# Hybrid RG-LRU / attention / RWKV-7 block: attention of the later queries first, and the output projection and feed-forward in the order of the later tokens

## Chip, cores and metric

One core of a Trainium2 chip. The metric is the device time in microseconds of one execution of the whole block. Engines: PE (TensorE), DVE (VectorE), ACT (ScalarE), POOL (GpSimd), SP (the queue that issues the DMAs).

## What is computed

One layer over 2048 tokens and 16 learned meta tokens ahead of them, width 1024:

```python
p = rms_norm(h, norm_mix_pre) @ w_in          # columns of three head groups
oa = rg_lru_group(...)                        # 256 columns, a recurrence over time
ob = forgetting_attention_group(q, k, v, f)   # 512 columns: 8 heads of 64, causal, with a decay bias
oc = rwkv7_group(...)                         # 256 columns, a recurrence over time
h = h + rms_norm(concat(oa, ob, oc) @ w_out, norm_mix_post)
f = causal_dwconv3(rms_norm(h, norm_ffn_pre) @ ffn_up); gate, val = split(f)
h = h + rms_norm((gelu(gate) * val) @ ffn_down, norm_ffn_post)
return h[:, 16:]
```

All arithmetic is float32; a product of two matrices is made of three products of split operands (`mm3`, L148 to L152).

## The kernel before

The order of each engine's instructions is set when the program is built: the code below is written in program order, a scheduler interleaves what is independent, and each engine then goes through its list in that order, waiting wherever an input isn't there.

Stages, in program order. The input projection (`psp`) runs with the RWKV and the LRU beside it; the RWKV isn't done when it ends, and goes on beside the attention. Its products are called `rps` and `eps`, and its lines are L898 to L1350.

Attention (`Attn`, L394) writes its queries as **steps**: one step is one head and one block of 512 queries. Block 0 sees 5 key tiles, block 1 sees 9, block 2 sees 13, block 3 sees 17 (the last tile of each has 16 keys, and the four tiles on the diagonal are narrower than 512). `run` (L708) goes through two halves: `half` 0 takes blocks 0 and 1 of all eight heads (short steps), `half` 1 takes blocks 2 and 3 (long steps), and `meta` (L537), the attention of the 16 meta tokens, stands between them. A head's keys (`keys`, L454, its DMAs on L469 to L476) are two float32 parts of the keys and the values. A short head needs 1040 key columns and fills half a slot of the ring of keys, so four short heads fit; a long head needs 2064 and fills a slot, so two fit. For each step, `maxima` (L479) makes the row maxima two steps ahead: PE product `mx` (L503), DVE reductions `mc` (L506, and L509 on the diagonal), then once a step the chain `sh` (L516, L517), a transposition (L521) and `q` (L532). `weights` (L597) then makes, for each pair of key tiles, the scores `sc` (L623, L624), the exponentials `p` on ACT (L626), the product with the values `po` (L635) and the sum `acc` on POOL and DVE (L656), and once a step the division by that sum (L675 to L688) with two trips through DRAM. `mx` has two PSUM banks, and a third once `wide` is set (`WIDE`, from head 5 of the first half).

The output projection (`w_out_tile`, L1377, products `pswo`) goes over 17 tiles of tokens (`FFN_TILES`, L1419: 2 tokens, which are the last meta tokens, then 16 times 128). A tile needs the attention of all heads for its tokens. Tiles 0 to 8 need meta tokens and blocks 0 and 1, tiles 9 to 16 blocks 2 and 3. In program order they stand behind the attention, but the scheduler moves tiles 0 to 6 into the long half. Tiles 7 and 8 (`HELD`) are kept until the last step but one. Each tile has one chain of small DVE operations (L84 to L89), L1412 and L1413 on DVE, and writes `scr_h`. From the ninth tile (`LATE`) each is followed by `ffn_norm` (L1440) of one tile of the first third of the feed-forward (products `pst`, copies L55 and L57), and after the last of these `ffn_sums` (L1473, 16 POOL subtractions on L1479) and the splits `xo` of its first three operands (L1484 on ACT, L1485 on DVE).

The up-projection (`ffn_up`, L1567, products `psu`) goes over three thirds of the tokens (`SUPERS`), 0, 1, 2, each with 22 column blocks; `between` (L1964) prepares the next third meanwhile. The down-projection (`psd`) goes over the tokens from the first to the last.

Of the kernel before, what the change touches and what calls it, by code (L numbers as in the profile page):

```python
# [29 lines left out]
NFF = FF // P  # L30
# [363 lines left out]
class Attn:  # L394
# [313 lines left out]
    def run(self):  # L708


        ready, self.steps = [], []
        for half, bs in enumerate(((0, 1), (2, 3))):
            if half:
                self.meta()
            for h in range(NH):
                self.wide = (half, h) >= WIDE
                keys = self.keys(h, 4 * bs[-1] + 5)
                for b in bs:
                    gen, total, out = self.maxima(h, b, keys), self.pieces(b), []

                    def fill(share, gen=gen, total=total, out=out):
                        while len(out) < min(total, share * total):
                            out.append(next(gen))

                    if len(ready) == self.AHEAD:
                        self.weights(*ready.pop(0), fill)
                        self.steps.append(self.last)
                    fill(1.0)
                    ready.append((h, b, keys, next(gen)))
        for step in ready:  # L730
            self.weights(*step, lambda share: None)
            self.steps.append(self.last)
        for _, _, f in self.later:
            f()
# [684 lines left out]
FFN_TILES = [(0, HALO)] + [(HALO + P * i, P) for i in range(SEQ // P)]  # L1419
# [2 lines left out]
HK = KD // 2  # L1422
SUPERS = 3

# [37 lines left out]
def ffn_quarters(core, pool, sup):  # L1462

    t = pool.tile([P, len(QUARTERS), HK, FN], F32, tag="q", name=core.n("q"))
    q = {s: t[:, i] for i, s in enumerate(QUARTERS)}
    used = SEQ + HALO - FBLK * (2 * sup + 1)
    if used < FN:
        for s in ("b0", "b1"):
            core.nc.gpsimd.memset(q[s][:, :, used:], 0.0)
    return q  # L1470


def ffn_sums(core, q, after=nullcontext):  # L1473

    q["t3"] = q["b0"]
    for k in range(HK):
        for o, x, y in (("t1", "b0", "a0"), ("t2", "b1", "t1"), ("t3", "b1", "b0"), ("t4", "a1", "t2")):
            with after():
                core.nc.gpsimd.tensor_tensor(q[o][:, k], q[x][:, k], q[y][:, k], op=ALU.subtract)  # L1479
            yield  # L1480
# [86 lines left out]
def ffn_up(core, raws, ring, pool, banks, w_up, cw, scr, between, tokens):  # L1567

    nc = core.nc
    tt, stt = nc.vector.tensor_tensor, nc.vector.scalar_tensor_tensor
    turn = 0
    units = [(sup, j) for sup in range(SUPERS) for j in range(NFF)]
    ahead = UpWeights(core, raws, ring, w_up, scr, 0)
    ws = [ahead.operand(i) for i in range(7)]
    xs = [tokens(0, i) for i in range(7)]

    def conv(src, u, j, n):
        y = pool.tile([P, FBLK], F32, tag="uy", name=core.n("uy"), bufs=UY)  # L1580
        cc = u * NFF + j
        nc.scalar.activation(y[:, :n], src[:, 2 : n + 2], AF.Copy, scale=cw[:, 88 + cc : 89 + cc])  # L1582
        for i in (1, 0):
            stt(y[:, :n], src[:, i : n + i], cw[:, 44 * i + cc : 44 * i + cc + 1], y[:, :n], op0=ALU.mult, op1=ALU.add)  # L1584
        if u == 0:
            nc.scalar.activation(y[:, :n], y[:, :n], AF.Gelu_apprx_tanh)
        return y

    def ending(g, v, j, b0, n):
        core.pooled = nc.gpsimd.tensor_tensor(v[:, :n], g[:, :n], v[:, :n], op=ALU.mult)  # L1590
        nc.sync.dma_start(scr["ff"][P * j : P * j + P, b0 : b0 + n], v[:, :n])

    for at, (sup, j) in enumerate(units):
        b0 = [FBLK * (2 * sup + i) for i in range(2)]
        n = [min(FBLK, SEQ - b) for b in b0]
        s = lambda tag: pool.tile([P, FN], F32, tag=tag, name=core.n(tag), bufs=1 if tag == "u2" else 2)[:]
        between(sup, j)
        more = at + 1 < len(units)
        if more:
            ahead = UpWeights(core, raws, ring, w_up, scr, units[at + 1][1])  # L1600
        ws_next, bank = [], {}
        turn ^= 1
        for i, (name, (_, _, at_)) in enumerate(PRODUCTS.items()):
            w, x = ws[i], xs[i]
            first = at_ not in bank
            if first:
                bank[at_] = banks[turn].tile([P, 512], F32, tag="up", name=core.n("psu"))[:, :FN]
            ps = bank[at_]
            for k in range(HK):
                mm3(nc, ps, w[:, 0, k], w[:, 1, k], x[:, 0, k], x[:, 1, k], first and k == 0, k == HK - 1, not first)  # L1610
            if j == NFF - 1 and more:
                xs[i] = tokens(sup + 1, i)
# [24 lines left out]
        ws = ws_next  # L1637
# [132 lines left out]
READY = 13  # L1770
PACE = 1.5

WIDE = (0, 5)

LATE = 8

HELD = 7, 8


class Beside:  # L1780
# [54 lines left out]
def hybrid_block_kernel(ctx: ExitStack, tc: tile.TileContext, args, out):  # L1835
    a = {s: v[0] if s != "meta_tokens" else v for s, v in args.items()}
    nc = tc.nc
    core = Core(tc, ctx)
    scr = scratch(tc, ctx, core)
# [4 lines left out]
    def run(gen):  # L1844
        for _ in gen:
            pass
# [78 lines left out]
    with ExitStack() as p3:  # L1925
# [12 lines left out]
        with p2:  # L1938
            ps_wo.append(pool(p2, "ps_wo2", 1, space=PSUM, **right))
            banks = Banks(core, ps_wo)  # L1940
            g_post = spread(pool(p2, "gpost", 1, **right), a["norm_mix_post"], "g_post")
            wp = pool(p2, "wp", 2, **right)
            w = w_out_load(core, wp, a["w_out"])
            todo = list(tiles[0])
            quarters = {0: ffn_quarters(core, qp, 0)}
            for i, (f, rows) in enumerate(FFN_TILES):
                with tc.issue_after(at.steps[-2].ins) if i in HELD else nullcontext():
                    _, rs[i] = w_out_tile(
                        core, wp, banks, scr, w, x, meta, g_post, f + META - HALO, rows, rsv[:, 6 * i : 6 * i + 6]
                    )  # L1950
                banks.wide = i >= LATE - 1
                if i >= LATE and todo:
                    q, f, rows = todo.pop(0)
                    ffn_norm(core, np_, ps_n, scr, f, rows, rs[q], g_fpre, quarters[0], 0)
                    if not todo:
                        run(ffn_sums(core, quarters[0]))
# [6 lines left out]

        def between(sup, j):  # L1964

            sup += 1
            if j == 1 and sup < SUPERS:
                quarters[sup] = ffn_quarters(core, qp, sup)
                todo[:] = tiles[sup]
            elif j == 1:  # L1970
                kept = qp.tile([P, DOWN_KEPT, 2, 512], F32R, tag="q", name=core.n("qd"))
                down.extend(kept[:, i] for i in range(DOWN_KEPT))
            elif sup == SUPERS:
# [89 lines left out]
```

## Time and profile before

| | |
|---|---|
| median of 3 runs | 3165.64 us (3157.63 to 3165.91) |
| the profiled execution | 3168.61 us, of it 3166.9 us span of the trace |
| granted TensorE clock | 0.958 |
| PE, DVE, ACT, POOL busy | 2955.7, 2196.1, 1446.3, 1274.0 us |
| input projection, first part of the RWKV | 0 to 918 us |
| attention beside the rest of the RWKV | 918 to 1228 us |
| attention, with output projection | 1228 to 1500 us |
| attention alone | 1500 to 1640 us |
| end of the attention, rest of the output projection | 1640 to 1795 us |
| up-projection | 1795 to 2670 us |
| down-projection | 2670 to 3167 us |

The stages are read from where the products of each name begin and end on PE. In the lines of the profile, `x` is a count, and what stands in brackets behind an instruction is how long its engine was idle ahead of it and who ended that.

### The profile page before, as it was taken

Reading aid. Unit: us, or ns where it says so; the run is one execution under the profiler, and the core shown is the slowest. Engines: PE = TensorE matmul, PEld = TensorE weight load, DVE = VectorE, ACT = ScalarE, POOL = GpSimd, SP = SyncE. Lnnn points to the kernel's source line nnn. Section 1 sums busy time; section 2 is a strip of 40 time slices with the busy share of each in tenths; the row PEclk is TensorE's granted clock in tenths of the full one; section 3 lists DMA queues with packets and bytes.
Section 4 is the critical chain, followed back from the end, with each engine's and each line's share of the span. In section 5 each row is a group of like instructions: output and inputs, shape, how many; then the busy total and the mean of one; then the engine's idle time right before and its main releaser. Section 6 shows DMA issues by size and latency. Waiting matters only on the chain. (4 is left out here: it accounts for less than half of the span.)

```text
span 3166.9 us, 52619 instructions
## 1 busy us (share of the span) xinstructions
PE 2955.7 (93%) x18488; PEld 2473.9 (78%) x18488; DVE 2196.1 (69%) x4563; ACT 1446.3 (46%) x2684; POOL 1274.0 (40%) x1426
## 2 busy tenths in 40 slices
PE   6988899999989998999999899999999999999998
PEld 6977788889965554554457699999999999787776
DVE  6147665766677777766657777787778787557777
ACT  3134323444444443434543456666666665324332
POOL 3334334211013444434651235433533334556665
PEclk9989899999987998999999899999999999999999
DMA  6777756643453344444326365555555565535444
GB/s 194 225 235 229 220 181 215 200 125 111 116 126 68 81 100 123 119 109 116 77 61 206 115 190 168 167 173 168 165 165 164 168 189 159 177 103 170 140 160 140
DMA packets 493817, 484.11 MB, mean 153 GB/s; under 512 B 83200, under 2 KB 408010, under 8 KB 487904
## 3 DMA queue, kind: packets, MB, share of 16 engines
q1 hardware_dynamic: 493168, 480.36, 50.8%
q8 instruction: 145, 2.38, 0.3%
q14 instruction: 120, 0.98, 0.1%
q0 software_dynamic: 384, 0.39, 0.0%
HBM read 354.76 MB, written 125.87 MB: 152 GB/s over the span
## 5 line engine op out<-in xcount | busy, mean ns | idle before, releaser
L150 PE MATMUL psu<-xo,uw 128*128 128x344 f32 x1848 | 588.7, 323 | 7.9 <-DVE wx L1413 4.8
L151 PE MATMUL psu<-xo,uw 128*128 128x344 f32 x1848 | 593.7, 322 | 1.0 <-DVE xo L1485 1.0
L152 PE MATMUL psu<-xo,uw 128*128 128x344 f32 x1848 | 583.0, 320 | 0.0
L150 PE MATMUL psp<-xh,wh 128*128 128x384 f32 (+2 forms) x1152 | 386.0, 335 | 0.0
L152 PE MATMUL psp<-xh,wl 128*128 128x384 f32 (+2 forms) x1152 | 382.1, 332 | 3.0 <-DVE wl L145 3.0
L151 PE MATMUL psp<-xl,wh 128*128 128x384 f32 (+2 forms) x1152 | 383.0, 332 | 0.0
L150 PEld LDWEIGHTS psu<-xo,uw 128*128 128x128 f32 x1848 | 347.5, 189 | 9.4 <-DVE wx L1413 5.2
L151 PEld LDWEIGHTS psu<-xo,uw 128*128 128x128 f32 x1848 | 348.9, 189 | 1.3 <-DVE xo L1485 1.3
L152 PEld LDWEIGHTS psu<-xo,uw 128*128 128x128 f32 x1848 | 347.2, 189 | 0.0
L1484 ACT ACTIVATE uw<-uq 128x512 fp32r<-128x512 f32 x462 | 287.0, 627 | 99.1 <-PE psu L152 48.0
L1485 DVE TENSOR_TENSOR uw<-uq,uw 128x512 fp32r<-128x512 f32 x330 | 283.2, 862 | 63.5 <-ACT uw L1484 58.6
L626 ACT ACTIVATE p<-sc,bias 128x512 f32<-128x512 f32 (+4 forms) x352 | 201.1, 592 | 267.8 <-PE sc L624 211.7
L1485 POOL TENSOR_TENSOR uw<-uq,uw 128x512 fp32r<-128x512 f32 x132 | 182.4, 1382 | 267.2 <-ACT uw L1484 233.8
L656 POOL TENSOR_TENSOR acc<-acc,p 128x512 f32<-128x512 f32 (+3 forms) x208 | 226.6, 1090 | 153.2 <-ACT p L626 118.8
L1584 DVE SCALAR_TENSOR_TENSOR uy<-psu,ffn_cols,uy 128x342 f32<-128x342 f32 (+1 forms) x396 | 224.2, 569 | 90.0 <-ACT uy L1582 88.9
L1590 POOL TENSOR_TENSOR uy<-uy,uy 128x342 f32<-128x342 f32 (+1 forms) x132 | 137.0, 1038 | 322.0 <-DVE uy L1584 133.9
L506 DVE TENSOR_REDUCE mc<-mx 128x1 f32<-128x400 f32 (+6 forms) x320 | 172.5, 554 | 93.4 <-PE mx L503 89.2
L152 PEld LDWEIGHTS psp<-xh,wl 128*128 128x128 f32 x1152 | 222.6, 193 | 10.3 <-issue 4.5
L150 PEld LDWEIGHTS psp<-xh,wh 128*128 128x128 f32 x1152 | 222.6, 193 | 8.8 <-issue 6.5
L151 PEld LDWEIGHTS psp<-xl,wh 128*128 128x128 f32 x1152 | 222.6, 193 | 6.5 <-issue 4.6
L1503 POOL TENSOR_TENSOR us<-us 128x512 f32<-128x512 f32 x88 | 131.3, 1492 | 222.3 <-DMA us<-in_ffn_up_dram 197.5
L1484 ACT ACTIVATE fo<-u 128x896 fp32r<-128x896 f32 x88 | 81.1, 922 | 234.3 <-POOL u L1700 117.1
(447 smaller groups left out, 6513.7 us busy)
## 6 DMA issues: line engine op xcount, KB each, us to landing
uq<-scr_us SPq DMA_DIRECT2D x264, 256.0 KB
uq<-in_ffn_up_dram SPq DMA_DIRECT2D x198, 256.0 KB
raw<-in_w_in_dram SPq DMA_DIRECT2D x72, 512.0 KB
us<-in_ffn_up_dram SPq DMA_DIRECT2D x44, 512.0 KB
scr_us<-us SPq DMA_DIRECT2D x22, 1024.0 KB
u<-scr_ff SPq DMA_DIRECT2D x88, 256.0 KB
scr_ff<-uy SPq DMA_DIRECT2D x110, 171.0 KB
q<-scr_qh SPq DMA_DIRECT2D x96, 128.0 KB
```

Of the source, the lines that this page charges most:

```text
L150: nc.tensor.matmul(out, ah, bh, start=first, stop=False, skip_group_check=more)
L151: nc.tensor.matmul(out, ah, bl, start=False, stop=False, skip_group_check=more)
L152: nc.tensor.matmul(out, al, bh, start=False, stop=last, skip_group_check=more)
L506: self.reduced = nc.vector.tensor_reduce(mc[:rows, i, ci : ci + 1], ps[:rows, :full], axis=AX.X, op=ALU.max)
L626: last = nc.scalar.activation(p[:rows, :w], ps[:rows, :w], AF.Exp, bias=bias[:rows, j : j + 1])
L656: eng.tensor_tensor(a, ps_[0][:rows, c0:n] if jj == 0 else a, p[:rows, : n - c0], op=ALU.add)
L1484: core.nc.scalar.activation(hi, src, AF.Copy)
L1485: (eng or core.nc.vector).tensor_tensor(lo, src, hi, op=ALU.subtract)
L1503: add, sub = (lambda o, x, y, op=op: nc.gpsimd.tensor_tensor(o, x, y, op=op) for op in (ALU.add, ALU.subtract))
L1584: stt(y[:, :n], src[:, i : n + i], cw[:, 44 * i + cc : 44 * i + cc + 1], y[:, :n], op0=ALU.mult, op1=ALU.add)
L1590: core.pooled = nc.gpsimd.tensor_tensor(v[:, :n], g[:, :n], v[:, :n], op=ALU.mult)
```

## The change

`run` takes the halves in the other order: first blocks 2 and 3 (long steps) of all heads, then the meta tokens, then blocks 0 and 1. The third bank for `mx` is used from the start of the second half. The output projection takes tiles 9 to 16 first, then 0 to 8; the two tiles that are kept for the end of the attention are now 15 and 16. The feed-forward takes its thirds in the order 2, 0, 1, so that the first third needs tiles 11 to 16 (six, where third 0 needs seven). The work, its shapes and the DMAs are the same in number.

```diff
-        for half, bs in enumerate(((0, 1), (2, 3))):
+        for half, bs in enumerate(((2, 3), (0, 1))):
...
+ORDER = 2, 0, 1
...
-    units = [(sup, j) for sup in range(SUPERS) for j in range(NFF)]
+    units = [(sup, j) for sup in ORDER for j in range(NFF)]
...
-WIDE = (0, 5)
+WIDE = (1, 0)
+OUT_ORDER = [9, 10, 11, 12, 13, 14, 15, 16, 0, 1, 2, 3, 4, 5, 6, 7, 8]
 LATE = 8
-HELD = 7, 8
+HELD = 6, 7
...
-            for i, (f, rows) in enumerate(FFN_TILES):
-                with tc.issue_after(at.steps[-2].ins) if i in HELD else nullcontext():
+            for at_, i in enumerate(OUT_ORDER):
+                f, rows = FFN_TILES[i]
+                with tc.issue_after(at.steps[-2].ins) if at_ in HELD else nullcontext():
...
-                if i >= LATE and todo:
+                if at_ >= LATE and todo:
```

What this does to the lists of the engines. First the start of the attention. On SP, before, behind the last stores of the input projection (`k` and `v` are the keys and values of the first head, `q` its queries):

```order
L469 DMA k_1494_10978<-scr_kh 64x1040
L473 DMA k_1493_10977<-scr_kh 64x1040
L474 DMA k_1493_10977<-scr_kl 64x1040
L471 DMA k_1494_10978<-scr_ch 1x1040
L472 DMA k_1494_10978<-scr_cl 1x1040
L475 DMA v_1495_10979<-scr_v 128x8x64
L476 DMA v_1495_10979<-scr_v 16x64
L490 DMA q_1496_10982<-scr_qh 64x512
L491 DMA q_1503_11006<-scr_qh 64x512
```

and now, at the same place:

```order
L469 DMA k_1494_10978<-scr_kh 64x2064
L473 DMA k_1493_10977<-scr_kh 64x2064
L474 DMA k_1493_10977<-scr_kl 64x2064
L471 DMA k_1494_10978<-scr_ch 1x2064
L472 DMA k_1494_10978<-scr_cl 1x2064
L475 DMA v_1495_10979<-scr_v 128x16x64
L476 DMA v_1495_10979<-scr_v 16x64
L490 DMA q_1496_10982<-scr_qh 64x512
L491 DMA q_1503_11006<-scr_qh 64x512
```

The order is the same; the keys and values ahead of the queries are twice as long. On PE at that place, as a difference (`rps` and `eps` are the RWKV's):

```order
 L990 MATMUL eps_8941<-rwsq_8804,bones 128x256
-L623 MATMUL sc_11101<-q_1503_11006,k_1493_10977 128x512
-L623 MATMUL sc_11107<-q_1503_11006,k_1493_10977 128x400
 L1222 MATMUL rps_8429<-ident,rww_903_6518 128x128 x2
 L1226 MATMUL rps_8432<-rwsg_6173,g_up 128x256
+L623 MATMUL sc_11149<-q_1503_11006,k_1493_10977 128x512
+L623 MATMUL sc_11154<-q_1503_11006,k_1493_10977 128x512
```

The first scores stand behind three small products of the RWKV, ahead of which they stood. Second, PE in the middle of the RWKV, around the same two of its products (L1145), before:

```order
L1130 MATMUL rps_10152<-rww_1228_8949,rwxf_9985 64x128 x4
L1145 MATMUL rps_10161<-rwsc_8948,rwxu_10130 64x128 x8
L503 MATMUL mx_11675<-k_1499_10989,q_1501_10993 128x256
L503 MATMUL mx_11680<-k_1499_10989,q_1501_10993 128x400
L623 MATMUL sc_11749<-q_1643_11428,k_1498_10988 128x144
L624 MATMUL sc_11749<-q_1492_10975,k_1499_10989 128x144
L635 MATMUL po_11648<-p_11718,v_1500_10990 64x512
L635 MATMUL po_11648<-p_11724,v_1500_10990 64x400
L623 MATMUL sc_11763<-q_1643_11428,k_1498_10988 16x16
L624 MATMUL sc_11763<-q_1492_10975,k_1499_10989 16x16
L1145 MATMUL rps_10172<-rwsc_8948,rwxu_10130 64x128 x8
```

and now:

```order
L1130 MATMUL rps_10152<-rww_1228_8949,rwxf_9985 64x128 x4
L1145 MATMUL rps_10161<-rwsc_8948,rwxu_10130 64x128 x8
L503 MATMUL mx_11554<-k_1494_10978,q_1501_10993 128x512
L624 MATMUL sc_11705<-q_1497_10986,k_1499_10989 128x512
L624 MATMUL sc_11710<-q_1497_10986,k_1499_10989 128x512
L503 MATMUL mx_11557<-k_1494_10978,q_1501_10993 128x256
L1145 MATMUL rps_10172<-rwsc_8948,rwxu_10130 64x128 x8
```

What stands between the two is now full key tiles of 512 in place of the narrow ones on the diagonal. Over the whole list, 121 key tiles (L623) of 52,224 columns in sum stand between the first of them and the RWKV's last product, where 110 of 37,728 columns stood. Third, DVE near the end of the output projection, around the split `xo` that needs the last POOL subtractions. Before:

```order
L1485 TENSOR_TENSOR xo_17867<-q_16212,xo_17867 128x1376
L88 SCALAR_TENSOR_TENSOR rs_3206_17466<-rs_3206_17466 128x1
L89 SCALAR_TENSOR_TENSOR rs_3206_17466<-rs_3206_17466 128x1
...
L1412 SCALAR_TENSOR_TENSOR pswo_17416<-pswo_17416,rs_3206_17466,g_post 128x512
L1412 SCALAR_TENSOR_TENSOR pswo_17441<-pswo_17441,rs_3206_17466,g_post 128x512
L1413 TENSOR_TENSOR wx_17414<-wx_17414,pswo_17416 128x512
L1413 TENSOR_TENSOR wx_17414<-wx_17414,pswo_17441 128x512
```

and now (the line numbers behind the change are 2 higher there):

```order
L89 SCALAR_TENSOR_TENSOR rs_3186_17264<-rs_3186_17264 128x1
L1412 SCALAR_TENSOR_TENSOR pswo_17214<-pswo_17214,rs_3186_17264,g_post 128x512
L1412 SCALAR_TENSOR_TENSOR pswo_17239<-pswo_17239,rs_3186_17264,g_post 128x512
L1413 TENSOR_TENSOR wx_17212<-wx_17212,pswo_17214 128x512
L1487 TENSOR_TENSOR xo_17854<-q_16212,xo_17854 128x1376
L1413 TENSOR_TENSOR wx_17212<-wx_17212,pswo_17239 128x512
```

The split stood ahead of a tile's L1412 and now stands behind it, ahead of the last L1413 only.

More of the change, by code (lines that the diff above doesn't have):

```diff
@@ L1573, in ffn_up @@
     turn = 0
-    units = [(sup, j) for sup in range(SUPERS) for j in range(NFF)]
+    units = [(sup, j) for sup in ORDER for j in range(NFF)]
     ahead = UpWeights(core, raws, ring, w_up, scr, 0)
     ws = [ahead.operand(i) for i in range(7)]
-    xs = [tokens(0, i) for i in range(7)]
+    xs = [tokens(ORDER[0], i) for i in range(7)]
     def conv(src, u, j, n):
@@ L1611, in ffn_up @@
             if j == NFF - 1 and more:
-                xs[i] = tokens(sup + 1, i)
+                xs[i] = tokens(units[at + 1][0], i)
             if more:
@@ L1950, in hybrid_block_kernel @@
                     )
[L1951 to L1952 removed]
+                banks.wide = at_ >= LATE - 1
+                if at_ >= LATE and todo:
                     q, f, rows = todo.pop(0)
[L1954 removed]
+                    ffn_norm(core, np_, ps_n, scr, f, rows, rs[q], g_fpre, quarters[ORDER[0]], ORDER[0])
                     if not todo:
[L1956 removed]
+                        run(ffn_sums(core, quarters[ORDER[0]]))
         ps_f.append(pool(p3, "ps_f1", 3, space=PSUM, **early))
@@ L1964, in between @@
         def between(sup, j):
-            sup += 1
-            if j == 1 and sup < SUPERS:
+            turn = ORDER.index(sup) + 1
+            sup = ORDER[turn] if turn < SUPERS else None
+            if j == 1 and turn < SUPERS:
                 quarters[sup] = ffn_quarters(core, qp, sup)
```

6 lines of the change are left out of this document (3 added, 3 removed).

## Prediction

> **What bounds the kernel now.** I read the page first, then the busy time of each stage, and then, inside the stages that the change touches, the waits of PE.
>
> ```profile
> span 3166.9 us, 52619 instructions
> PE 2955.7 (93%) x18488; PEld 2473.9 (78%) x18488; DVE 2196.1 (69%) x4563; ACT 1446.3 (46%) x2684; POOL 1274.0 (40%) x1426
> PEclk9989899999987998999999899999999999999999
> ```
>
> PE is busy 93% of the span. By stage (length, then busy time of PE, PEld, DVE, ACT, POOL, granted clock, DMA share):
>
> ```profile
> 918.00:1228.00 310.00, 274.59 (x2316) 169.02 (x2315) 237.54 (x770) 128.15 (x274) 122.02 (x215) 0.85 0.39 91
> 1228.00:1500.00 272.00, 248.83 (x1004) 138.22 (x1004) 194.17 (x485) 118.35 (x203) 119.77 (x132) 0.95 0.50 125
> 1500.00:1640.00 140.00, 133.71 (x540) 63.05 (x539) 89.77 (x203) 71.13 (x119) 91.92 (x107) 0.98 0.29 67
> 1640.00:1795.00 155.00, 137.19 (x599) 104.70 (x598) 103.42 (x273) 52.55 (x102) 31.94 (x32) 0.94 0.46 153
> 1795.00:2670.00 875.00, 871.33 (x5525) 870.01 (x5525) 673.83 (x1080) 550.05 (x1076) 351.46 (x295) 1.00 0.55 168
> 2670.00:3167.00 497.00, 459.16 (x1970) 368.10 (x1968) 333.34 (x513) 171.60 (x278) 295.43 (x374) 0.98 0.46 152
> ```
>
> In every stage PE leads, so an order alone can win only two things: the time in which PE is idle, and the time in which its clock is granted at half. Beside the RWKV (918 to 1228) the idle time is 310 - 274.6 = 35.4 us and the clock is 0.85, worth 0.15 x 310 = 46 us at most. In the next two stages together idle is 23.2 + 6.3 = 29.5 us. The up-projection has none to win, and the down-projection comes after everything that is moved and keeps its order: both stay, 1372 us. What is left is 918 to 1795.
>
> **The change, part by part.** Work is conserved, so each term is idle time or clock. How much attention lies where (PE, weight loads and ACT of the scores; two matmuls are one key tile), and the output projection:
>
> ```profile
> 918.00:1228.00 310.00, 61.50 (x224) 35.86 (x224) 56.28 (x110) 0.85 0.39 91
> 1500.00:1640.00 140.00, 62.08 (x206) 31.33 (x206) 62.27 (x104) 0.98 0.29 67
> 1228.00:1500.00 272.00, 88.44 (x336) 57.43 (x336) 18.66 (x28) 9.47 (x28) 0.95 0.50 125
> ```
>
> Alone, 103 long tiles take 140 us, 1.36 us each. A mean long tile has 431 columns (12,928 a head over 30 tiles), so a column costs 3.16 ns. The changed list puts 52,224 columns beside the RWKV instead of 37,728: 14,496 x 3.16 ns = 46 us of attention move ahead of the RWKV's end, and 46 us leave the part behind it. That is no gain as such; it is one only as far as it fills idle time.
>
> *A, the start.* The first scores wait for keys and queries:
>
> ```profile
> 927.04 1.10 PE L623 MATMUL sc<-q,k 128*128 128x512 f32 x2 [8.43 <-DMA q<-scr_ql]
> 920.00:925.00 5.00, 0.00 (x0) 0.00 (x0) 4.50 (x15) 0.35 (x1) 1.09 (x2) 0.50 1.11 197
> k<-scr_kh SPq DMA_DIRECT2D x8, 260.0 KB
> k<-scr_kh SPq DMA_DIRECT2D x8, 516.0 KB
> ```
>
> Three key parts grow by 256 KB each, the values likewise: 1.02 MB more ahead of the queries, at 197 GB/s 5.2 us. Of it the three products of the RWKV that now stand ahead hide about 1.6 us (1.1 us stand as the length of the pair of 512 in the row above; they are of its size): **+3.6**, between 0 and +6.
>
> *B, the waits for keys.* A long head's slot comes free only one step before its next keys are needed. The waits that the profile lays to keys in 1250 to 1500 and in 1500 to 1640:
>
> ```profile
> PE mx L503 <- DMA k<-scr_cl: 8.3, 2, 4.4
> PE mx L503 <- DMA k<-scr_cl: 3.1, 2, 2.3
> ```
>
> Four waits, 11.4 us, 2.85 each; of six reloads two are hidden. Now no output projection stands beside the long half, and four of the six reloads stand on SP among the RWKV's DMAs. All six at 2.85 are 17.1: **+6**, between 0 (the RWKV's products cover them) and +15 (4.4 each).
>
> *C, idle time beside the RWKV.* Without the start it is 35.4 - 8.4 = 27 us. Its largest waits:
>
> ```profile
> PE sc L623 <- ACT p L626: 3.8, 5, 2.1
> PE rps L1081 <- DVE rwxu L1111: 3.6, 3, 2.0
> PE rps L1222 <- DVE rww L1215: 2.3, 1, 2.3
> PE po L635 <- DVE o L667: 2.3, 1, 2.3
> PE mx L503 <- DVE q L532: 2.0, 4, 1.0
> PE rps L1043 <- DVE rwbk L1037: 1.7, 1, 1.7
> ```
>
> L667 and L532 come once a step, and eight steps run here instead of sixteen; the RWKV's own waits have more PE work between them. With 38% more columns (52,224 / 37,728) on the same RWKV I take a third off: **-9**, between 0 and -20.
>
> *D, the clock.* Three stretches after the start (columns as in the stages):
>
> ```profile
> 960.00:964.00 4.00, 2.01 (x34) 1.78 (x33) 3.86 (x10) 1.41 (x2) 0.60 (x2) 0.50 0.57 106
> 964.00:978.00 14.00, 14.00 (x91) 10.95 (x91) 10.96 (x34) 9.05 (x19) 4.74 (x10) 0.50 0.15 45
> 978.00:992.00 14.00, 14.00 (x50) 7.79 (x50) 3.91 (x14) 4.67 (x10) 4.57 (x5) 0.50 0.11 29
> ```
>
> A wait of 2 us is followed by 28 us at half clock though PE is never idle in them: 14 us lost by one wait. With a third fewer waits I take a fifth of the 46 us: **-9**. The ends are -30 (the 0.95 of the next stage, 0.05 x 310 = 15.5 left) and +14 (one more such stretch). [...]
>
> *E, the short half beside six output tiles.* Its DVE work per step is the question, for the row of the short steps is dense with it (16 steps, 930 to 1225):
>
> ```profile
> L506 DVE TENSOR_REDUCE mc<-mx 128x1 f32<-128x400 f32 (+7 forms) x108 | 51.3, 481 | 13.7 <-PE mx L503 10.5 <-DMA rwia<-da 2.4 <-PE sc L624 0.2
> L509 DVE CUSTOM_DVE_ANT_0 mj<-mx,future 128x128 f32<-128x128 f32 x67 | 18.4, 278 | 4.0 <-PE mx L503 3.9
> L532 DVE TENSOR_TENSOR q<-mx,ident 4x512 fp32r<-4x512 f32 x16 | 10.9, 682 | 3.9 <-PE mx L521 3.6
> L667 DVE TENSOR_TENSOR o<-po,oh 64x400 f32<-64x400 f32 (+1 forms) x15 | 9.1, 606 | 1.0 <-ACT o L666 1.0
> L687 DVE TENSOR_TENSOR o<-o,rb 64x512 f32<-64x512 f32 x12 | 8.8, 733 | 2.7 <-DMA rb<-scr_rden 2.7
> L656 DVE TENSOR_TENSOR acc<-acc,p 16x16 f32<-16x16 f32 (+1 forms) x22 | 7.5, 342 | 1.5 <-POOL acc L656 1.5
> L517 DVE TENSOR_SCALAR sh<-sh,cref 128x4 f32<-128x4 f32 x16 | 6.2, 389 | 0.3
> ```
>
> These are 112 us. An output tile takes DVE at most (194.2 - 125 x 89.8 / 103) / 7 = 12 us (125 key tiles lie in 1228 to 1500; the rest is seven output tiles and the weights' split), six take 73. So DVE needs about 185 us. PE needs 37,888 columns x 3.16 ns = 120 us and 6 x 48 products x 88.44 / 336 = 76 us, with the idle share of 1228 to 1500 (23.2 / 272) 214 us. DVE would be at 86%, against 71% in that stage: it fits, with less slack. **+5**; below, -4 if the slack suffices and short steps wait less for ACT; above, +26, if DVE gets no further than the 237.5 / 310 = 77% that it has beside the RWKV (185 / 0.77 = 240).
>
> *F, the end of the output projection.* On DVE the split `xo` waits for POOL's subtractions, and a tile's L1412 waits behind it:
>
> ```profile
> 1737.84 14.94 POOL L1479 TENSOR_TENSOR q<-q 128x344 f32<-128x344 f32 x12 [4.21 <-DVE q L57]
> 1752.71 1.58 DVE L1485 TENSOR_TENSOR xo<-q,xo 128x1376 fp32r<-128x1376 f32 x1
> 1757.16 0.79 PE L150 MATMUL pswo<-woh,mh 128*128 128x512 f32 x1 [6.00 <-DVE wx L1413]
> ```
>
> The split now stands behind L1412 and one L1413. Only the other L1413 and the next tile's inputs wait, about half as long; one `ffn_norm` fewer stands here and one more in the up-projection, which has none to hide it. **-3**, between -7 and +3. At the end of the attention nothing is gained: two tiles are held as before, and tile 0, which needs the meta tokens alone, follows them.
>
> Sum: 3.6 + 6 - 9 - 9 + 5 - 3 = **-6.4 us**. The profiled execution took 3168.6 us (span 3166.9 and 1.7 around it), so 3162.2; the median shown lies 3.0 below it, which gives **3159 us**, 0.2% less. About 0.3%, 9.5 us, is what a measurement of this kernel can tell from no change.
>
> **The rivals.**
>
> *The RWKV's gaps are really filled.* 20 of the 27 us of idle time go, and the clock rises to 0.95 (-30): 3.6 + 6 - 20 - 30 + 5 - 3 = -38, 3127 us. For it speaks that both losses sit in that stage; against it, that PE is already busy 89% of it and the start, where most of the half clock lies, doesn't get better.
>
> *Slower: DVE bounds the short half.* Place: behind the long half, beside the six output tiles. Price: +26 instead of +5, sum +15, and 3181 us; with C and D at nothing, 3199. It decides once DVE can't be used over 185 / 214 = 86%. For it speaks that PE follows DVE once a step through L532 and that the third bank doesn't help DVE; against it, that the output projection needs no answer from DVE within a step.
>
> *The half clock isn't bound to load.* Stretches like 964 to 992 come again whatever stands beside: D is 0, 3168 us. [...]
>
> **How the numbers follow.** Forecast (-20 to +10 around 3159): 0.38, of it 0.15 faster by over 0.3%, 0.21 within, 0.02 slower. Gaps filled: 0.20, faster. DVE bound: 0.33, slower. Clock not bound to load: 0.09, of it 0.07 within, 0.02 slower. So faster 0.35, within 0.28, slower 0.37. The forecast's own range is 3146 to 3176; with the two large rivals, whose prices lie 30 us below and 22 to 40 above, 3120 to 3196.
>
> **What would show it.** A: the first L623 waits about 12 us instead of 8.4. B: six waits of `mx` for `k`. C and D: in the stage up to the last `rps` idle time near 25 us in all and a clock of 0.88, in a stage some 25 to 40 us longer. E: between the first `pswo` and the last `po`, DVE at 86%, and waits of PE for L532, L506 and L667 that stay under 20 us. F: a wait for L1413 of 3 us where 6.0 stood. The forecast is wrong if the up- or down-projection change by over 3 us, or if SP holds the keys back by far more than 4.4 us a head.

## The result, and the profile after

The changed kernel took 3184.78 us (median of 5 runs, 3181.78 to 3197.85) against 3165.64 us (5 runs): ratio 1.0075, interval 1.005 to 1.010. It is slower by 0.75%; 3159 us and slightly faster had been forecast. A second set, seven runs of the same kernel beside 21 of the kernel before on another chip, gave 1.0078 (1.005 to 1.0105); an eighth, of 3217.88 us, counts as slow and is left out here and below.

The page of the changed kernel, its span, busy times and clock:

```profile
span 3183.1 us, 52601 instructions
PE 2977.4 (94%) x18488; PEld 2482.9 (78%) x18488; DVE 2199.5 (69%) x4563; ACT 1444.9 (45%) x2684; POOL 1267.1 (40%) x1426
PEclk9989899999977889999999899999999999999999
```

PE is busy 22 us longer than before with the same 18,488 products, and around the RWKV the clock's digits read 77889, where they read 87998. Next the stages, cut where the products of each name begin and end (input projection to 905, RWKV to 1250, first output tile at 1462, last `po` at 1675, first `psu` at 1807, last `psu` at 2704; columns as in the prediction):

```profile
905.00:1250.00 345.00, 305.06 (x2312) 185.76 (x2313) 254.05 (x675) 135.04 (x263) 141.39 (x185) 0.82 0.31 68
1250.00:1462.00 212.00, 183.17 (x715) 81.81 (x714) 131.68 (x323) 95.47 (x159) 120.74 (x138) 0.93 0.46 113
1462.00:1675.00 213.00, 208.61 (x906) 125.23 (x906) 141.68 (x475) 92.56 (x188) 86.98 (x147) 0.98 0.46 121
1675.00:1807.20 132.20, 114.93 (x507) 87.05 (x506) 96.38 (x255) 42.31 (x81) 19.10 (x19) 0.96 0.49 161
1807.20:2703.80 896.60, 893.45 (x5641) 891.38 (x5642) 693.46 (x1111) 562.58 (x1100) 357.41 (x308) 0.99 0.55 170
2703.80:3183.10 479.30, 445.60 (x1873) 353.70 (x1872) 323.04 (x495) 161.71 (x261) 286.30 (x360) 0.97 0.45 149
```

The kernel before, cut at the same products. (Ahead of the prediction its up-projection was said to end at 2670; its last `psu` ends at 2686.)

```profile
915.00:1223.80 308.80, 274.47 (x2316) 168.67 (x2314) 235.76 (x771) 127.56 (x273) 120.88 (x213) 0.85 0.39 92
1223.80:1248.20 24.40, 16.38 (x57) 7.63 (x55) 16.33 (x40) 8.16 (x14) 7.54 (x11) 0.81 0.81 193
1248.20:1682.00 433.80, 410.13 (x1674) 223.05 (x1675) 290.06 (x713) 196.84 (x338) 219.48 (x248) 0.97 0.39 99
1682.00:1791.40 109.40, 91.59 (x406) 72.96 (x406) 83.09 (x209) 35.00 (x67) 20.20 (x17) 0.92 0.53 176
1791.40:2685.90 894.50, 890.38 (x5633) 888.77 (x5634) 687.45 (x1108) 562.51 (x1099) 361.07 (x311) 1.00 0.55 170
2685.90:3166.90 481.00, 443.72 (x1874) 352.93 (x1872) 321.80 (x496) 162.14 (x261) 286.03 (x359) 0.98 0.45 148
```

The up- and down-projection differ from before by about 2 us each, with opposite signs, and the input projection (whose PE order is the same) took 904 us here and 915 in the profile before. What is between them, from the last product of the input projection to the first of the up-projection, went from 876 to 903 us.

The new stage is the second row: 212 us of long steps with nothing beside them, since the RWKV is done and no output tile is ready. PE is idle 28.8 us of it (14%); the long steps that stood alone before had 6.3 us in 140. The third row is the opposite: the short steps beside output tiles leave 4.4 us idle, and DVE is at 67%. Together the two have 33.2 us idle, where the attention behind the RWKV had 8.0 + 23.7 = 31.7 before: what the short half saves, the new stage loses. The waits of PE in the second row:

```profile
PE mx L503 <- DVE mc L506: 7.4, 6, 1.6
PE po L635 <- ACT p L626: 6.8, 6, 3.8
PE sc L623 <- ACT p L626: 4.2, 6, 1.3
PE mx L521 <- DVE mc L496: 3.4, 4, 1.8
PE mx L503 <- DVE q L532: 2.5, 5, 0.7
PE mx L503 <- DMA k<-scr_kl: 0.8, 1, 0.8
```

Of the 28.8 us, 13.3 are waits of the maxima for DVE (`L503` and `L521`) and 11.0 are waits for the exponentials on ACT. The maxima wait for their own reductions, 7.4 us in six waits in the first row: the program gives `mx` two PSUM banks here, and its next product waits until DVE has emptied one of them. The keys, for which I had added 6 us, cost 0.8.

### The profile page after: what moved, and what is told of

It is laid out like the page before. It is cut to its first block, busy times and chain, and to the rows that moved or that the text cites. A ratio compares the mean times of both kernels' runs of the same rounds, so it can differ in the third digit from the quotient of the medians.

```text
span 3183.1 us, 52601 instructions
## 1 busy us (share of the span) xinstructions
PE 2977.4 (94%) x18488; PEld 2482.9 (78%) x18488; DVE 2199.5 (69%) x4563; ACT 1444.9 (45%) x2684; POOL 1267.1 (40%) x1426
## 5 line engine op out<-in xcount | busy, mean ns | idle before, releaser
L506 DVE TENSOR_REDUCE mc<-mx 128x1 f32<-128x400 f32 (+4 forms) x320 | 174.3, 557 | 99.0 <-PE mx L503 92.1
L635 PE MATMUL po<-p,v 128*64 128x512 f32 (+4 forms) x704 | 178.0, 552 | 14.3 <-ACT p L626 12.8
```

Of the source, the lines that this page charges most:

```text
L506: self.reduced = nc.vector.tensor_reduce(mc[:rows, i, ci : ci + 1], ps[:rows, :full], axis=AX.X, op=ALU.max)
L635: mm = nc.tensor.matmul(po[64 * i : 64 * i + 64, c0:n], v1[:rows, j], p[:rows, : n - c0], start=jj == 0, stop=jj + i + 2 >= len(kt), tile_ ...
```

## The experiments

Theory 1: the loss sits in the stage with nothing beside it, since two banks bound the long steps there. Its rivals: the half clock beside the RWKV (2), or long steps that wait for DVE and ACT whatever the banks (3).

Each kernel ran beside the kernel before on the same chip. "Beyond the clock" is worked out as follows. Over the 229 executions with a recorded time and clock, an execution that loses 1 us more by the granted clock ((1 - clock) x span) than another of the same kernel has a span 0.58 us longer. With that share taken out of the mean span, and the mean of the 96 executions of before subtracted, what is left is the time that the clock doesn't explain (some 3 us uncertain). The last column is PE's idle time from the last product of the input projection to the first of the up-projection, in the one profile of each kernel (three of the changed kernel).

| kernel | ratio to before (interval) | mean clock | beyond the clock | PE idle, by profile |
|---|---|---|---|---|
| before | 1 | 0.9565 | 0 | 83.8 us |
| changed, 13 executions | 1.0075 and 1.0078 | 0.9558 | +18 us | 90.6, 98.4, 97.7 |
| changed, third bank from head 5 of the long half | 1.0059 (1.0039 to 1.0078) | 0.9521 | +12 | 92.1 |
| from head 4 | 1.0000 (0.9982 to 1.0018) | 0.9568 | -2 | 75.7 |
| from head 3 | 0.9998 (0.9981 to 1.0014) | 0.9571 | 0 | 81.7 |
| from head 2 | 1.0036 (1.0015 to 1.0057) | 0.9549 | +9 | 90.0 |
| changed, queries ahead | 1.0065 (1.0046 to 1.0085) | 0.9550 | +17 | 91.4 |
| changed, one tile more early | 1.0028 (1.0011 to 1.0045) | 0.9590 | +12 | 91.1 |
| changed, third bank from head 3, one tile more early | 0.9974 (0.9955 to 0.9994) | 0.9577 | -6 | 79.8 |
| these two and the queries ahead | 1.0040 (1.0024 to 1.0055) | 0.9571 | +13 | 92.6 |
| before, third bank never | 1.0091 (1.0074 to 1.0108) | 0.9547 | +28 | 99.0 |
| before, from the second half | 0.9979 (0.9965 to 0.9993) | 0.9578 | -4 | 85.0 |
| before, from head 3 | 1.0063 (1.0042 to 1.0083) | 0.9493 | +7 | 88.0 |
| before, long steps of heads 0 to 3 first | 1.0035 (1.0018 to 1.0052) | 0.9563 | +9 | 93.7 |

The last two columns go together: the kernels with at most 85 us idle stand between -6 and 0, those with 88 or more between +7 and +28. So what the clock doesn't explain lies in PE's waits in this part, as far as one profile of each can say.

**Where the third bank of the maxima begins.** `WIDE = (half, head)`; before (0, 5), in the change (1, 0). The first trial:

```diff
-WIDE = (1, 0)
+WIDE = (0, 5)
```

> The changed kernel with the third bank of the maxima from head 5 of the first (long) half, near the end of the RWKV, in place of the start of the short half. Theory 1 (two banks bound the part of the long half that has neither RWKV nor output projection beside it): its idle time of PE, 28.8 of 212 us, falls to about 10 and its clock rises from 0.93 to 0.97; 3184.8 - 25 = about 3160 us, ratio to before 0.998. Theory 2 (the loss is the half clock beside the RWKV): at most 5 us, ratio 1.006. Theory 3 (with nothing beside them the long steps wait for DVE and ACT whatever the banks): idle stays over 25 us, ratio 1.006.

Measured 1.0059. The stage with nothing beside it and the one behind it (195 and 226 us; this profile is of the slowest of its twelve executions):

```profile
1270.60:1465.60 195.00, 180.36 (x732) 84.17 (x732) 130.98 (x324) 97.83 (x162) 120.87 (x140) 0.93 0.54 128
1465.60:1691.90 226.30, 208.87 (x911) 128.85 (x911) 147.30 (x475) 93.44 (x190) 89.19 (x149) 0.98 0.44 114
```

Idle time fell from 28.8 to 14.6 us, as theory 1 had it, but the next stage had 17.4 us idle where 4.4 had stood: the gain came back as waits there, most of them for DVE (`mx` for `q` 3.6 us, the output projection for `wx` 3.4). So theory 1 was right on the stage and wrong on the total, and the question was whether the place was wrong.

With `WIDE = (0, 3)`:

> The changed kernel with the third bank of the maxima from head 3 of the long half (its PSUM bank is free once the recurrences' gate products eps are done, some 110 us before the RWKV ends). Theory 1' (the long steps lack the bank beside the RWKV too, and a wait for the maxima's reduction is what drops the clock there): the waits of mx for L506 and L509 go, idle beside the RWKV 40 to 46 us falls by 4, the clock loss there (62, 63, 74 us in three profiles) falls to about 45; behind it 15 us of idle where 29 stood; ratio 0.998 to 1.002. Against it (as with the bank from head 5, idle time that goes in one stage comes back in the next): ratio 1.005 to 1.007.

Measured 0.9998: the whole loss is gone. But not as theory 1' had it: the clock loss beside the RWKV was 72.8 us in its profile, no less than in the others. What did come as expected is the idle time behind the RWKV, 14.1 us. With `WIDE = (0, 4)`:

> The changed kernel with the third bank from head 4: between head 3 (0.9998) and head 5 (1.0059). If the price of the missing bank grows smoothly with the heads that lack it: 1.002 to 1.004. If what counts is that the maxima get ahead while the RWKV still runs (from head 3, 129 score tiles stand ahead of the RWKV's last product; from head 4 119, from head 5 121): 1.005 or more.

Measured 1.0000, better than both expectations. As many score tiles stand ahead of the RWKV's last product here as in the trial from head 5, so the lead beside the RWKV isn't what counts. Its two stages (this profile is of the fastest of its twelve executions, 3149 us where the median is 3173):

```profile
1243.40:1435.30 191.90, 178.96 (x761) 84.01 (x761) 136.40 (x338) 101.87 (x169) 129.70 (x153) 0.97 0.55 131
1435.30:1640.90 205.60, 200.80 (x876) 121.19 (x875) 138.30 (x462) 89.15 (x182) 84.93 (x138) 0.99 0.47 125
```

and PE's waits in the first of them:

```profile
PE mx L503 <- DMA k<-scr_cl: 3.4, 2, 1.8
PE sc L623 <- ACT p L626: 2.6, 6, 0.8
PE mx L503 <- DVE mc L506: 1.7, 5, 0.8
PE mx L521 <- DVE mc L496: 0.7, 1, 0.7
PE po L635 <- ACT p L626: 0.3, 1, 0.3
```

The waits for the reduction fell from 7.4 to 1.7 us, those of `L521` from 3.4 to 0.7, and those of `po` for ACT from 6.8 to 0.3. Idle time is 12.9 us here and 4.8 in the next stage, so this time nothing came back. Why the trial from head 5 gave its gain back isn't settled, nor how a bank for the maxima shortens the wait of `po`.

With `WIDE = (0, 2)`:

> The changed kernel with the third bank from head 2 of the long half. From head 3 it measured 0.9998, from head 5 1.0059, from the short half 1.0075. If each head more with the bank is worth some 2 to 4 us: 0.998 to 0.999. If at head 2 the bank isn't free yet (its PSUM bank belongs to the gate products until about 2/3 of the RWKV), maxima wait for it on PE in order, and it is 1.002 or more.

Measured 1.0036: worse than from heads 3 and 4. In its profile the stage with nothing beside it has 14.1 us idle, but the next has 16.1 where 4.4 stood: the gain came back there as it did from head 5. Why isn't settled either.

The same line in the old order. Never a third bank (`WIDE = (2, 0)`):

> The kernel before without the third bank. Theory 1: idle of PE in the part of the long half that stands alone rises from 4.5% to about 13% of it (6 to 19 us of 140), beside the output projection by less; in all +12 to +20 us, ratio 1.004 to 1.006. Theory 3: the output tiles and the ACT waits set the pace, ratio 1.000 to 1.002.

Measured 1.0091, more than theory 1 had. From the first output tile to the last `po`:

```profile
1230.40:1725.00 494.60, 451.18 (x1778) 243.27 (x1778) 306.56 (x773) 205.93 (x357) 232.33 (x258) 0.96 0.39 96
PE mx L503 <- DVE mc L506: 8.6, 10, 1.6
```

43.4 us idle instead of 23.7, with the same wait in it. The first output tile comes sooner here; counted from the end of the RWKV it is 45.4 against 31.7. Long steps need the bank in either order. Now the line of the change alone, `WIDE = (1, 0)` in the kernel before:

> The kernel before with only the line on the third bank as the change has it: from the start of the second half instead of head 5 of the first. In the old order the second half starts with the RWKV's end, so two banks are left to three heads of short steps beside the RWKV alone. If the price of that line hangs on what stands in the stretch (216 us of bare long steps in the new order): 1.000 to 1.003 here, where the whole change measured 1.0075. If the line costs the same wherever it stands: 1.005 to 1.008.

Measured 0.9979: slightly faster. So that line is no loss as such; it is one where 216 us of long steps stand ahead of the second half. And earlier than before, `WIDE = (0, 3)`:

> The kernel before with the third bank from head 3 instead of head 5 of its short half. If the bank helps short steps beside the RWKV as it helps long ones: 0.996 to 0.998, and the new order is still behind the old one. If three heads of short steps don't gain by it, or the bank isn't free: 1.000 to 1.003, and the two orders at their best bank are equal.

Measured 1.0063, against both expectations; 14 of its 20 us go with the clock (0.9493, 24 us more lost, times 0.58). So of the places tried, the best one for the bank is not the same in the two orders.

**The clock beside the RWKV.** Two profiles of the changed kernel lose 62 and 63 us of clock there, that of the kernel before 46 ((1 - clock) x length). Is it the order?

> The changed kernel unaltered, a second profile. If the lost clock beside the RWKV is set by the order, the loss from the last product of the input projection to that of the RWKV is again 55 to 68 us (before: 49) and the stage about 343 us; if it is chance, it may be 49 or less and the stage 330. The input projection, whose order the change does not touch, shows how far a stage differs between executions: 905 to 916 us.

The stage was 350.4 us at clock 0.82. That spoke for the order, until profiles of other kernels with the same instructions in that stage came in. The same wait of PE, in the changed kernel and in the one with one tile more (whose order there is the same), and the 25 us behind it:

```profile
1062.48 0.45 PE L503 MATMUL mx<-k,q 128*128 128x400 f32 x1 [1.55 <-DVE mc L506]
1068.00:1093.00 25.00, 25.00 (x146) 17.24 (x145) 14.36 (x51) 7.54 (x20) 4.04 (x9) 0.52 0.17 38
```

```profile
1083.49 0.45 PE L503 MATMUL mx<-k,q 128*128 128x400 f32 x1 [1.55 <-DVE mc L506]
1086.00:1111.00 25.00, 25.00 (x248) 16.77 (x246) 20.28 (x69) 12.74 (x30) 11.11 (x16) 1.00 0.19 44
```

The wait is 1.55 us both times. In one execution the clock falls 6 us behind it, with PE busy in between, and PE makes 146 products in 25 us; in the other it doesn't, and PE makes 248. Five of the kept profiles have this order: in four the clock falls here, between 0.7 us ahead of the wait's end and 6 us behind it, and in the fifth it doesn't. Whether the wait or the small products around it bring the fall isn't shown. The two kernels with the bank from head 3 show what such falls are worth. Up to the end of the RWKV their order is the same:

```profile
909.30:1273.20 363.90, 324.22 (x2360) 195.86 (x2358) 267.78 (x707) 140.38 (x271) 147.97 (x191) 0.80 0.33 69
```

```profile
908.50:1254.40 345.90, 304.55 (x2359) 181.97 (x2358) 266.72 (x707) 139.66 (x271) 148.54 (x191) 0.87 0.35 73
```

18 us between two executions of one order. So the profile of one execution can't tell whose the clock is; all executions can:

> The changed kernel unaltered, in five rounds beside the kernel before on one chip. If the order itself loses clock (term D with the other sign), the mean granted clock of its executions lies under that of the kernel before by 0.003 or more (10 us of 3180), as in the two profiles (0.955 and 0.953 against 0.958). If the loss is chance from execution to execution, the two means agree within 0.0015, and the ratio is again 1.005 to 1.010 for reasons other than the clock.

The mean clock was 0.9557 against 0.9568 for the kernel before: within 0.0015, as expected if the loss is chance. With all 13 executions of the changed kernel it is 0.9558 against 0.9565 (96 executions): 3 us more lost, 2 us of time. That is the clock's part in the 20 us by which the mean spans differ; 18 us are left. Still, the third profile of the changed kernel lost 63 us beside the RWKV again, so that the order loses some clock in that stage isn't excluded.

Does it depend on the kind of work how long the half clock lasts? The first score product made twice in the first eight steps:

```diff
+                if len(self.steps) < 8:
+                    nc.tensor.matmul(ps[:rows, :w], k1[:, ks : ks + rows], q1[:, c0:n], start=True, stop=True)
                 nc.tensor.matmul(ps[:rows, :w], k1[:, ks : ks + rows], q1[:, c0:n], start=True, stop=False)
```

> The changed kernel, with the first product of each score tile made twice in the first eight steps (the first one is overwritten by the second): about 106 more products of 0.40 us, 42 us of dense work on PE beside the RWKV. Theory 2a (a fallen clock stays at half as long as the RWKV's small products make up most of PE's work): the clock loss beside the RWKV (61 us) falls under 40 and idle time by some 5; about +15 us, 3200 us, ratio 1.011. Theory 2b (the stretches at half clock have nothing to do with the kind of work): the products cost 42 / 0.82 = 51 us, less 5 of idle time: 3231 us, ratio 1.021.

Measured 1.0103 (1.0081 to 1.0125), and for the stage beside the RWKV, first in this kernel, then in the second profile of the changed one:

```profile
910.20:1262.70 352.50, 315.38 (x2395) 196.13 (x2394) 250.72 (x662) 131.21 (x255) 135.48 (x176) 0.85 0.30 63
```

```profile
911.30:1261.70 350.40, 304.19 (x2300) 185.05 (x2299) 252.16 (x673) 132.31 (x261) 139.52 (x183) 0.82 0.30 65
```

Some hundred products more cost 11 us of busy PE and 2 us of stage, with 10 us less clock lost (53 against 63). That leans to theory 2a, though the loss didn't fall under its 40; but two executions of one order differ by as much, so it isn't shown.

**Long steps of four heads only.** The kernel before, with the long steps of heads 0 to 3 ahead, then all short steps, then the other long steps:

```diff
-        for half, bs in enumerate(((0, 1), (2, 3))):
+        units = [(high, h) for h in range(4)] + [(low, h) for h in range(NH)] + [(high, h) for h in range(4, NH)]
+        for u, (bs, h) in enumerate(units):
...
+                self.wide = u >= 5
```

> The kernel before with only one thing moved: the long steps of heads 0 to 3 come first, beside the RWKV, then all short steps, then the long steps of heads 4 to 7 beside the output projection; output projection and feed-forward in their old order. If the loss sits beside the RWKV (theory 2: clock +15 us, start +5, idle): the stage is again 340 to 350 us with 60 us of clock lost, ratio 1.006 to 1.010. If it sits in the bare long steps of heads 4 to 7 and in the 25 us of output projection that move behind the attention: these are gone, the short steps alone have DVE at 75% and idle below 15 us, and the ratio is 0.997 to 1.002.

Measured 1.0035 (1.0018 to 1.0052), between the two. Its stages: beside the RWKV, short steps with nothing beside them, long steps with output tiles:

```profile
909.40:1236.60 327.20, 283.73 (x2292) 172.06 (x2290) 248.41 (x672) 132.57 (x259) 138.24 (x179) 0.87 0.34 72
1236.60:1412.20 175.60, 154.33 (x643) 72.37 (x642) 120.63 (x372) 83.30 (x159) 91.98 (x157) 0.87 0.57 143
1412.20:1689.30 277.10, 266.73 (x1112) 155.62 (x1112) 179.23 (x479) 114.86 (x208) 115.24 (x134) 1.00 0.38 99
```

Long steps stand beside the RWKV as in the change, and the stage loses 42.5 us of clock, less than before (this profile is of one of its faster executions, 3171.7 where the median is 3181.9). What is left bare is now short steps, with the third bank from the second of their heads on, and it still has 21.3 us idle in 175.6, 10.0 of them waits of `L623` for ACT. So the third bank doesn't free every bare stage of its waits.

**The start.** The first queries ahead of the second key operand and the values of the first head:

```diff
+        def rest():
             nc.sync.dma_start(k1f[0:64, :n], scr["kh"][r, :n])
...
+                    if self.kept and self.kept[0]:
+                        out.append(next(gen))
+                        self.kept[0]()
```

> The changed kernel with the first queries ahead of the first head's second key operand and values on SP. Term A (the longer keys delay the start by about 5 us): idle time in the 45 us behind the input projection falls from 20 to 15 us, in all -5 us, ratio 1.006 where the changed kernel has 1.0075. If the start is bound by what the RWKV waits for (its inputs behind 2 MB of keys): no change, ratio 1.0075.

Measured 1.0065 (1.0046 to 1.0085), which by the time tells neither from the other. The 45 us behind the input projection, in the kernel before, the changed one, and this one:

```profile
915.00:960.00 45.00, 31.30 (x274) 21.65 (x272) 35.12 (x108) 15.09 (x32) 12.95 (x21) 0.69 0.84 179
```

```profile
903.80:948.80 45.00, 23.38 (x152) 16.45 (x150) 30.40 (x85) 9.69 (x19) 6.42 (x8) 0.66 0.84 172
```

```profile
911.10:956.10 45.00, 26.98 (x248) 20.27 (x246) 30.95 (x83) 9.70 (x19) 6.15 (x6) 0.62 0.86 169
```

Idle time 13.7, 21.6 and 18.0 us. The DMA engines are at 84% or more in all three. PE's longest wait there, with the queries ahead (line numbers are 12 higher in this kernel):

```profile
PE rps L1234 <- DVE rww L1227: 9.6, 1, 9.6
```

That is as long as without the edit (9.5 at `L1222`), and the wait for the queries behind it is gone. So what holds PE at this place is the RWKV's own input, as the second expectation had it.

**One output tile more beside the short steps** (`HELD = 7, 8`):

> The changed kernel with one more output tile free to go beside the short steps (positions 7 and 8 kept for the end instead of 6 and 7). Both stages have PE nearly always busy, so 5 us of products only change place: ratio 1.0075, within 0.002. If the tile fills idle time or the tail has slack to win: -3 to -5 us, 1.006.

Measured 1.0028 (1.0011 to 1.0045), a larger gain than expected. But the mean clock of its executions was 0.959; beyond the clock it stands at +12 us, against +18. With the bank from head 3:

> The changed kernel with the third bank from head 3 and one more output tile beside the short steps, the two edits that measured best alone (0.9998, and 1.0028 against 1.0075). If the tile's gain is real, 0.996 to 0.998. If it was the clock (the executions of that kernel had a mean granted clock of 0.959 where the changed kernel had 0.957), the two together give 0.999 to 1.000.

Measured 0.9974: faster than both kernels. Against the bank alone that is 0.24%, of which the mean clocks (0.9577 and 0.9571) explain little; the two intervals overlap, so the tile's share is likely, not shown. And with the queries ahead as well:

> The changed kernel with the three edits together: third bank from head 3, one more output tile beside the short steps, the first queries ahead of the first head's second key operand and values. Bank and tile alone measured 0.9974. If the 8 us of idle time that the start gained (21.6 of the 45 us behind the input projection, where 13.7 stood) come back by the earlier queries, 0.995 to 0.996; if the start is bound by what the RWKV waits for, 0.997 to 0.998.

Measured 1.0040: worse, and in no expectation. The 45 us behind the input projection:

```profile
915.80:960.80 45.00, 22.93 (x248) 17.15 (x246) 30.21 (x81) 9.59 (x19) 6.15 (x6) 0.75 0.85 171
```

22.1 us idle, as without the edit: this edit didn't win the 8 us back. From input to up-projection PE is idle 92.6 us where 79.8 stood without it; the edit at the start had changed the order of what follows. The stage beside the RWKV took 364 us where the two edits without it took 346, but the bank alone, with the same order as those two there, took 364 as well, so that stage's time says little.

## Why the prediction was wrong

**The step that failed in the sum is C and D.** The prediction took 18 us from the longer steps beside the RWKV, 9 of idle time and 9 of clock. Measured are about 0 and a loss of some 2. Without these two, the other terms as forecast come to +11.6, a slower kernel. By the rows, PE's idle time from input to up-projection went from 83.8 us to 90.6 (98.4 and 97.7 in two further profiles): +8 at the start, -2 to +4 in the rest of the RWKV's stage, +1.5 to +4 in the attention behind it, nothing in the tail.

**A second step is missing from the sum.** The change moves the third bank of the maxima from head 5 of the first half to the start of the second. The prediction priced the RWKV's stage, the short half and the tail, and named the bank only to say that it doesn't help DVE in the short half. Between the RWKV's end and the first output tile lie four heads of long steps, some 216 us. They had no term, though the row that would have priced it was quoted: 140 us of long steps alone, with three banks, had 6.3 us idle. With two banks idle is 28.8. With the bank from head 3 or 4 of the same order the kernel takes as long as before (0.9998, 1.0000), so moving this one line wins the whole 0.75% back. The bare stage is where the new order's gain went: with the bank from head 4 the attention behind the RWKV has 12.9 + 4.8 = 17.7 us idle, without it 33.2, in the old order 31.7. How the bank does it is shown for head 4, in part, by the waits that go (7.4 to 1.7, 6.8 to 0.3). That the total follows the stage isn't a law: from heads 2 and 5 the stage gained as much and the next one lost most of it, and why stays open.

**A, the start:** +3.6 forecast, 0 to 6 as bounds. Idle time in the 45 us grew by 7.9 us (13.7 to 21.6; 21.7 and 22.1 in two further profiles): direction right, size beyond the bound. The delay itself was priced well: the first scores start 17.2 us behind the input projection where 11.7 stood, 5.5 us later (5.2 forecast), and the wait ahead of them is 9.5 + 2.9 us where 8.4 stood. Most of it now falls to `L1222`, which the new list has ahead of the scores; its input `rww` is ready 12.6 us behind the input projection in both kernels. The other 4 us are waits further on, 2.8 of them for one of the recurrences' products at `L1315`, which the sum didn't count.

```profile
916.84 0.66 PE L1222 MATMUL rps<-ident,rww 128*128 128x128 f32 x2 [9.50 <-DVE rww L1215]
```

**B, the keys:** +6 forecast; 0.8 us measured where 11.4 stood. With the bank back from head 4 the wait in that stage is 3.4. Likely the maxima with two banks were late enough for the keys to be there; no run isolates it.

**C, idle beside the RWKV:** -9 forecast. Without the first 45 us it was 20.6 before, and 18.5, 24.6 and 20.9 in three profiles of the changed kernel: nothing gained. That longer steps fill gaps was a guess by a ratio of columns.

**D, the clock:** -9 forecast, about +2 us of time measured over all executions. The rival "the half clock isn't bound to load" was nearest. The +15 us of lost clock beside the RWKV that the two first profiles show would have looked like its refutation; that the same order loses the clock near the wait of 1.55 us in some executions and keeps it in another says why they don't settle it. The premise, 14 us lost by one wait, was misread as well: in the kernel before the clock falls at 959.1, and the wait of 2 us begins at 962.0, so it doesn't start that stretch (the row from 960 to 964 has 0.50 throughout).

**E, the short half:** forecast 214 us with DVE at 86%. It took 210 to 214 with DVE at 66 to 67%, and idle 4.4 to 4.7. The length came out by luck: PE was busy 208.6 us where 196 were forecast, and idle 4.4 where 18 were. The rival "DVE bounds the short half" gives 3181 us, close to the 3184.8 measured, by a mechanism that didn't occur: DVE had 141 us of work there, not 185. The lines that the prediction adds up to 112 took 90, since the maxima of only 13 of the 16 short steps stand in this stage. The number was met by accident.

**F, the tail:** -3 forecast, 0 measured (idle 17.8 before, 17.3 after). The place is as the order had it, the wait isn't shorter:

```profile
1739.24 1.58 DVE L1487 TENSOR_TENSOR xo<-q,xo 128x1376 fp32r<-128x1376 f32 x1
1748.06 1.42 DVE L1412 SCALAR_TENSOR_TENSOR pswo<-pswo,rs,g_post 128x512 f32<-128x512 f32 x2
1750.12 0.80 PE L150 MATMUL pswo<-woh,mh 128*128 128x512 f32 x1 [7.22 <-DVE wx L1413]
```

The last split no longer stands ahead of `L1412`, but an earlier one does, and the tile's chain of small operations begins behind it. PE waits 7.2 us where 6.0 stood.

Some 25 us of output projection moved behind the attention (507 products in that stage against 406). By the idle time of the tail that cost nothing.

## What to carry to other kernels

When an order is reversed, look for every constant that is tied to a place in the old order (here: from which head on a buffer may be used), find what stands at that place now, and price it in each stage, above all in the stages that the new order makes and the old one didn't have. A stage in which one loop runs with nothing beside it is priced by the row where that loop ran alone, with its buffers as they were there. A gain put in as a share of a total (a third of the waits, a fifth of the lost clock) is a guess until a row or a run shows one. And where a profile shows a difference in clock, compare the granted clock of many executions before giving it a cause.

## What the runs showed of the hardware

The clock is lost in steps. In the clock records of the two kernels, and where the other profiles were read microsecond by microsecond, every stretch at half clock behind the input projection and ahead of the up-projection that is seen whole lasts a multiple of 3.41 us: 3.4, 6.8, 10.2 and so on, 34.1 in the kernel before (from 959.1) and 37.6 with the bank from head 3 (from 911.6) among them. In these readings stretches over 15 us occur only before the RWKV's end, where its small products stand among the attention's (82 on 64x64 weights from 1068 to 1093 in the changed kernel, 32 on 32x32 weights at 960.1 in the kernel before). In that row of the changed kernel PE is busy 25 of 25 us, at 0.52: the clock stays at half for 23.9 us from 1068.5 on, though PE has no idle time in them. What decides whether the clock falls near a wait of 1.55 us isn't shown here. That the small products hold it down leans on one run (the score product made twice); it isn't shown.

Two executions of one order differed by 18 us in one stage at nearly the same idle time (39.7 and 41.4 us), so by the clock, and two kernels with the same order up to the end of that stage (bank from head 5, one tile more) had mean clocks of 0.952 and 0.959 over twelve and ten executions. I can't say what fixes that mean.
